# Spreading the first norm's weight row by a product, and loading and splitting the first projection's pieces in another order

## The chip, the cores and the metric

The kernel runs on one core of one Trainium2 chip. The metric is device time in microseconds of one execution; the median of several executions is compared. Lower is better.

## What is computed

A decoder trunk of two layers on 256 tokens of 1024 channels, in float32, with a final norm:

```
h = x
for i in range(2):
    hn = rmsnorm(h, ln_mix[i])
    parts = split(hn @ w_in[i])
    mix = concat(delta_rule(parts), sparse_attention(parts), stick_breaking(parts))
    h = h + mix @ w_out[i]
    h = h + conv_ffn(rmsnorm(h, ln_ffn[i]))
    h = h + sigmoid(rmsnorm(h, ln_ple[i]) @ w_ple_gate[i]) * rmsnorm(p[i] @ w_ple[i], ple_norm[i])
return rmsnorm(h, ln_final)
```

Here `rmsnorm(x, w)` is x times (mean of x² + 1e-6) to the power -1/2, times the weight row w. The change lies in the first norm of the first layer and in the first product behind it.

## The kernel before

Tokens lie on the partitions, in two tiles of 128 (`h[:, 0]` and `h[:, 1]`). Every large product is made of two summands for each operand in the format float32r: the high one is a rounded copy (written by ScalarE, `wh_...`, `XH`), the low one what is left (by VectorE, `wl_...`, `XL`), and three products of the four are summed in PSUM: high by high, low weights by XH, high weights by XL.

Weights stream in pieces (`PIECES`) through SyncE's DMA queue into five buffers (`prefetch`, L506; `WR`, L384). `split_step` (L537) splits half a piece at a time: an activation to `hi`, a subtraction to `lo`. A buffer is free, and the next piece's load is issued, when a piece is split. The first four pieces of a layer are `g1` (`wr_g` in the profile, 414 KB each, two of the eight k-tiles of the first projection each); three pieces `k` and two `kcvc` follow.

`setup` (L612) issues the first transfers on SyncE in this order: x's first tile in two halves, 160 columns of constants (the identity for the transposes among them), the weight row of the first norm spread over 128 partitions (`row(0)`, L680, 512 KB), two pieces, x's second tile, the positions, and the pieces that still have a buffer. `warm` (L632) issues products of zeros, whose results nobody reads; `WARM` holds their numbers: 12 at the start, 2 behind the first transposes, 3, 5, 5 and 0 behind the products of the four pieces.

`main` (L1774) then writes the first norm down: `norm_stats` squares a tile on ScalarE and takes (sum + eps) to the power -1/2 on GpSimd (`ssq`), `norm_mul` (L718) multiplies h by it and by the row on VectorE (`xh`), `norm_T` (L767) transposes four k-tiles on TensorE and splits them to `XH` and `XL`. `split_to(n)` stands between these steps and so sets where the pieces' splits stand on ScalarE's and VectorE's queues. `proj` (L852) takes the first projection for tile 0 of the tokens: for each piece the products with XH, then behind all four those with XL; then `second()` brings tile 1's transposes, and the same is done for tile 1.

The order of all instructions is fixed when the program is built. Each engine takes its own in order. In the mixers (the three mixers' streams) a rough model of the engines' clocks (`Model`, L191) picks what is written next, so a change of what stands ahead also changes how the streams are woven later. All computing instructions have line L307, that of the helper that records them; so they are told apart by the names of their tiles.

Of the kernel before, what the change touches and what calls it, by code (L numbers as in the profile page):

```python
# [18 lines left out]
T = 256  # L19
D = 1024  # L20
# [8 lines left out]
LAG = 2  # how many steps of the feed-forward the down-projection runs behind  # L29
LAST = 4  # pieces of the down-projection at the end, through which the tiles of tokens go one after the other  # L30
PG = [NJ - 11, NJ - 9, NJ - 7, NJ - 5]  # the steps of the feed-forward that the first pieces of the last gate come with
# the mixers' outputs (0: delta rule, 1: stick-breaking, 2: sparse) in the order in which each layer's output projection takes them
GROUPS = ((2, 0, 1), (2, 0, 1))
TILES = (3, 2, 3)  # their sizes

# columns of w_in, as the reference splits them
# [5 lines left out]
def _pieces():  # L42
    """The pieces in which the weights of a layer stream in: name, [k, columns]. w1k and w1v are used as they are."""
# [23 lines left out]
# columns of per-channel parameters  # L67
# [8 lines left out]
# columns of constants  # L76
# [8 lines left out]
CC_F = CC["lev"][0]  # from here on they are wanted in bfloat16 only  # L85
# [51 lines left out]
def _prep(inp):  # L137
    """Lays the arrays out: the weights in the order in which they stream, parameters of channels as columns."""
# [14 lines left out]
    for l in range(DEPTH):  # L153
# [16 lines left out]
        for n, i, k, c in PIECES:  # L170
            a = whole[n]
            per = a.shape[1] // k  # pieces along the contraction
            ki, ci = (i % per, i // per)
            ws.append(np.ascontiguousarray(a[:, ki * k:ki * k + k, ci * c:ci * c + c]).reshape(-1))
# [16 lines left out]
class Model:  # L191
    """A rough clock of each engine, from which the order of the instructions is chosen as they are written down."""

    HOP = {"pe": 0.2, "act": 0.16, "dve": 0.16, "pool": 0.12}
    WINDOW = 4096 / 1200  # us
    BUSY = 3060  # columns of all rows

    def __init__(self):
        self.clock = {"pe": 0.0, "dve": 0.0, "act": 0.0, "pool": 0.0}
        self.ready = {}  # L200
        self.used = {}
        self.loaded = 2.0  # when the loads so far have passed
        self.grids, self.fresh, self.banks = {}, {}, {}
        self.part = None  # the tile of tokens that is worked on
        self.parted = set()  # tensors that are followed by tiles of tokens
        self.cols = {}  # columns that the tensor engine's array passed in each window of its clock's gate

    def keys(self, names):
        """What a tensor is known by: its parts, where it is followed in parts."""
# [8 lines left out]
    def slow(self, t):  # L218
        """Whether the array runs at half its rate at a time."""
        return self.cols.get(int(t / self.WINDOW) - 1, 0.0) < self.BUSY  # L220

    def behind(self):
        """Whether the array has been too idle in this window to keep its rate in the next."""
# [4 lines left out]
    def region(self, ap):  # L228
        """When each element that an operand covers was written and was last used, as views: [half of the partitions, ...]."""
        t = ap.tensor  # L230
        if t.name not in self.grids:
            n = int(np.prod(t.shape[1:]))
            self.grids[t.name] = g = np.zeros((2, 2, n))  # (ready, used)
# [10 lines left out]
    def load(self, ap, cost):  # L244
        """A load of a piece of weights."""
# [4 lines left out]
    def op(self, eng, cost, outs, ins, cols, oaps, iaps):  # L250
# [7 lines left out]
        for b in banks:  # one engine at a time  # L258
# [24 lines left out]
class Engine:  # L283
    """Passes instructions on and counts what they cost."""
# [26 lines left out]
    def cost(self, op, out, ins, kw):  # L311
        n = max([out.free_size()] + [a.free_size() for a in ins])
        if self.n == "pe":
# [4 lines left out]
            if dt == F32:  # products for different halves of the columns run side by side in part  # L318
# [19 lines left out]
class Pool:  # L338
    """A pool of tiles whose model knows when their places were last used."""
# [19 lines left out]
class Halves:  # L359
    """One summand of a piece in several tiles, one behind the other along the contraction."""  # L360
# [8 lines left out]
class Need:  # L369
    """What a stream waits for: banks of PSUM, tiles or flags, a time."""  # L370
# [5 lines left out]
class Trunk:  # L376
    # How each layer's streams are woven together. pace: the share of columns below which the projections go first, early: how
    # long the array waits for what is more urgent, slack: how far ahead of the products the pieces are split, beside the mixers
    # and beside the feed-forward, step: k-tiles between two looks at what is more urgent; the rest: the streams' urgency.
# [4 lines left out]
    WR = 5  # pieces loaded ahead  # L384
    WARM = (12, 2, 3, 5, 5, 0)

    def __init__(self, ctx, tc, I, out, tap=None, depth=DEPTH):
# [13 lines left out]
        self.WS = 4  # pieces in two summands at a time  # L401
# [8 lines left out]
        # weights  # L410
# [6 lines left out]
        self.hold = False  # no split now: the engines have something more urgent  # L417
# [86 lines left out]
    # Pieces that are used as they are go where the mixers have nothing yet.  # L504
# [32 lines left out]
    AHEAD = (0, 1, 1, 2, 2, 1, 1, 0)  # pieces that are split behind each part of the last gate  # L537
    HALF = 512

    def split_step(self):  # L540
        """Splits half of the next piece into two float32r summands; false where there is no room."""
# [20 lines left out]
        self.a.activation(part(hi), src[:, s], AF.Copy)  # L562
        self.v.tensor_sub(part(lo), src[:, s], part(hi).bitcast(F32))
# [1323 lines left out]
```

## Time and profile before

| | |
|---|---|
| median of three runs | 847.37 us |
| lowest, highest | 846.48, 849.69 us |
| profiled execution: its span, from the first to the last instruction | 844.7 us |
| profiled execution: its own time | not stated apart; the median lies 2.7 us above the span |
| instructions | 17700 |
| TensorE, VectorE, ScalarE, GpSimd busy | 98%, 75%, 57%, 9% |
| mean granted clock of TensorE | 0.995 of full |

The profile is one execution. A row of the timeline gives start and duration in us from the start of the span, the engine (PE is TensorE, PEld its weight loads, DVE VectorE, ACT ScalarE, POOL GpSimd, SP SyncE; a q behind it is the engine's queue), the operation, the tile written and those read, and in brackets the idle time of the engine before it and what ended that. PE is "busy" whenever a product is in it, one of zeros too. PEclk is the granted clock of TensorE as a share of 2.4 GHz; 0.50 is 1.2 GHz.

### The profile page before, as it was taken

How to read it: one execution, taken by the hardware profiler on the slowest of the kernel's cores; microseconds unless marked ns; L12 is line 12 of the kernel's file. 1: busy time of each engine (PE TensorE's matmuls, PEld its weight loads, DVE VectorE, ACT ScalarE, POOL GpSimd, SP SyncE). 2: the span in 40 equal slices, each digit the busy share in tenths (PEclk: the TensorE clock that was granted, in tenths of full speed). 3: DMA queues.
4: the chain of work that ended last, by engine and by line, in shares of the span. 5: the costliest groups of instructions: out<-in, count | busy, mean ns of one | idle time of the engine just before them, and what ended most of it. 6: DMA issues, size and time to landing. Idle time of an engine off the chain costs nothing.

```text
span 844.7 us, 17700 instructions
## 1 busy us (share of the span) xinstructions
PE 827.0 (98%) x7007; PEld 742.9 (88%) x7007; DVE 633.3 (75%) x1305; ACT 480.7 (57%) x1043; POOL 77.1 (9%) x147
## 2 busy tenths in 40 slices
PE   8999999999999999999999999999999999999996
PEld 4987888987999999998999888897889999999986
DVE  4777987676887788877675688967588877878755
ACT  4546565565765566654655365637466656656543
POOL 1130001121100000000311100031110000000012
PEclk9999999999999999999999999999999999999998
DMA  8853221314575566753466133213355656766511
GB/s 283 298 189 100 77 75 41 104 58 144 198 232 191 188 211 215 224 187 120 127 227 224 34 126 102 64 52 101 126 174 196 206 197 194 215 216 213 177 35 50
DMA packets 37683, 130.71 MB, mean 155 GB/s; under 512 B 4576, under 2 KB 5088, under 8 KB 37600
## 3 DMA queue, kind: packets, MB, share of 16 engines
q1 hardware_dynamic: 36144, 124.66, 45.0%
q0 software_dynamic: 1312, 4.72, 1.7%
q8 instruction: 55, 0.90, 0.4%
q14 instruction: 28, 0.23, 0.1%
q10 hardware_dynamic: 144, 0.20, 0.1%
HBM read 128.51 MB, written 1.05 MB: 153 GB/s over the span
## 4 chain that ended last, share of the span: by engine, by line
PE 92%; ACT 3%; DMA 2%; DVE 1%; issue 0%; POOL 0%; SPq 0%; POOLq 0%; DVEq 0%; ACTq 0%
PE b L307 92%; DMA wr_w1k<-in_w_dram 1%; DMA row<-in_rows_dram 1%; ACT XH L307 1%; DMA wr_w1v<-in_w_dram 0%; DVE wl_g L307 0%; ACT L425 0%; ACT L L307 0%; ACT xh L307 0%; DVE xh L307 0%; DVE ck L307 0%; ACT cv L307 0%; POOL ssq L307 0%; ACT th L307 0%; ACT P L307 0%
## 5 line engine op out<-in xcount | busy, mean ns | idle before, releaser
L307 DVE SCALAR_TENSOR_TENSOR u<-b,pc,u 128x255 f32<-128x255 f32 (+1 forms) x176 | 84.7, 481 | 41.3 <-ACT u L307 38.2
L307 PE MATMUL b<-XL,wh_up 128*128 128x256 f32 x352 | 99.7, 283 | 0.0
L307 PE MATMUL b<-XH,wl_up 128*128 128x256 f32 x352 | 99.6, 283 | 0.0
L307 PE MATMUL b<-XH,wh_up 128*128 128x256 f32 x352 | 99.6, 283 | 0.0
L307 PE MATMUL b<-XH,wh_ga 128*128 128x256 f32 x352 | 99.0, 283 | 0.0
L307 PE MATMUL b<-XH,wl_ga 128*128 128x256 f32 x352 | 99.0, 283 | 0.0
L307 PE MATMUL b<-XL,wh_ga 128*128 128x256 f32 x352 | 97.2, 283 | 0.0
L307 ACT ACTIVATE u<-b,pc 128x256 f32<-128x256 f32 x88 | 41.6, 472 | 74.9 <-PE b L307 74.9
L307 PE MATMUL b<-wh_dn,al 128*128 128x512 f32 x176 | 69.4, 394 | 0.0
L307 PE MATMUL b<-wl_dn,ah 128*128 128x512 f32 x176 | 69.3, 394 | 0.0
L307 PE MATMUL b<-wh_dn,ah 128*128 128x512 f32 x176 | 69.2, 393 | 0.0
L307 PEld LDWEIGHTS b<-XH,wh_ga 128*128 128x128 f32 x352 | 66.9, 190 | 1.7
L307 PEld LDWEIGHTS b<-XL,wh_ga 128*128 128x128 f32 x352 | 65.9, 190 | 1.5
L307 PEld LDWEIGHTS b<-XL,wh_up 128*128 128x128 f32 x352 | 67.1, 191 | 0.0
L307 PEld LDWEIGHTS b<-XH,wh_up 128*128 128x128 f32 x352 | 67.1, 191 | 0.0
L307 PEld LDWEIGHTS b<-XH,wl_up 128*128 128x128 f32 x352 | 67.1, 191 | 0.0
L307 PEld LDWEIGHTS b<-XH,wl_ga 128*128 128x128 f32 x352 | 66.9, 190 | 0.1
L307 DVE TENSOR_TENSOR wl_ga<-wr_ga,wh_ga 128x512 fp32r<-128x512 f32 x88 | 56.9, 688 | 6.2 <-ACT wh_ga L307 2.6
L307 DVE TENSOR_TENSOR wl_up<-wr_up,wh_up 128x512 fp32r<-128x512 f32 x88 | 56.6, 685 | 0.4
L307 DVE TENSOR_TENSOR wl_dn<-wr_dn,wh_dn 128x512 fp32r<-128x512 f32 x88 | 56.6, 684 | 0.4
L307 ACT ACTIVATE ah<-sg 128x256 fp32r<-128x256 f32 x44 | 18.4, 419 | 64.7 <-DVE sg L307 64.7
L307 ACT ACTIVATE wh_up<-wr_up 128x512 fp32r<-128x512 f32 x88 | 50.3, 621 | 0.0
(371 smaller groups left out, 2243.0 us busy)
## 6 DMA issues: line engine op xcount, KB each, us to landing
wr_ga<-in_w_dram SPq DMA_DIRECT2D x44, 512.0 KB, 4.1
wr_up<-in_w_dram SPq DMA_DIRECT2D x44, 512.0 KB, 4.2
wr_dn<-in_w_dram SPq DMA_DIRECT2D x44, 512.0 KB, 3.8
wr_out<-in_w_dram SPq DMA_DIRECT2D x16, 512.0 KB, 3.5
wr_pg<-in_w_dram SPq DMA_DIRECT2D x16, 512.0 KB, 4.0
wr_g<-in_w_dram SPq DMA_DIRECT2D x8, 512.0 KB, 6.4
row<-in_rows_dram POOLq DMA_DIRECT2D x8, 512.0 KB, 4.2
wr_g<-in_w_dram SPq DMA_DIRECT2D x8, 414.0 KB, 5.0
```

The costliest lines, as they stand in the source:

```text
L307: return f(*args, **kw)
```

## The change

The row of the first norm is loaded as one row of 4 KB on one partition, by GpSimd's queue. A matrix product of a column of 128 ones by that row, one for each half of its columns, spreads it over the partitions in two banks of PSUM, which `norm_mul` then reads. The constants move from SyncE's queue to ScalarE's. All four pieces of `g1` are issued ahead of x's second tile. Products of zeros are left at two places: 3 at the start, 4 behind the two row products. The first piece is split by VectorE (high) and GpSimd (low), ahead of the first `norm_mul`; the second piece behind it, the third behind tile 0's transposes, the fourth behind tile 1's squares. In `proj` the products of the first three pieces with XL come ahead of those of the fourth piece with XH.

```diff
-    WARM = (12, 2, 3, 5, 5, 0)
+    WARM = (3, 4)
...
-    def split_step(self):
+    def split_step(self, hi_on=None, lo_on=None):
...
-        self.a.activation(part(hi), src[:, s], AF.Copy)
-        self.v.tensor_sub(part(lo), src[:, s], part(hi).bitcast(F32))
+        if hi_on is None:
+            self.a.activation(part(hi), src[:, s], AF.Copy)
+        else:
+            hi_on.tensor_copy(part(hi), src[:, s])
+        (lo_on or self.v).tensor_tensor(part(lo), src[:, s], part(hi).bitcast(F32), op=OP.subtract)
...
+        r0 = cp.tile([1, D], F32, tag="row", name="row0")
+        self.gdma(r0, I["rows"][0:1])
         for s in self.HS:
             self.sync.dma_start(self.h[:, 0, s], I["x"][0:128, s])
         cst = cp.tile([128, CC_F], F32, name="cst")
-        self.sync.dma_start(cst[:, 0:160], I["const"][:, 0:160])
-        self.row(0)
-        self.prefetch(2)
+        self.adma(cst[:, 0:160], I["const"][:, 0:160])
+        self.prefetch(4)
         self.sync.dma_start(self.h[:, 1], I["x"][128:256])
...
+        ones = self.gp.tile([1, 128], F32, tag="S", name="ones", bufs=2)
+        v.memset(ones, 1.0)
         self.warm(0)
+        self.row0 = [self.bank("row0") for _ in self.HS]
+        for b, s in zip(self.row0, self.HS):
+            self.t.matmul(b, ones, r0[:, s], start=True, stop=True)
+        self.n_row = 1
+        self.warm(1)
...
         for s in cols:
-            self.v.scalar_tensor_tensor(xh[t][:, s], self.h[:, t, s], sq[:, 0:1], row[:, s], op0=OP.mult, op1=OP.mult)
+            gains = row[s.start // 512] if isinstance(row, list) else row[:, s]
+            self.v.scalar_tensor_tensor(xh[t][:, s], self.h[:, t, s], sq[:, 0:1], gains, op0=OP.mult, op1=OP.mult)
...
         for t in range(2):
+            late = 0
             for i in range(4):
                 if t == 0:
                     Ws.append(self.take("g1", i))
+                if i == 3:
+                    yield self.need(0, self.of(t))
+                    for late in range(3):
+                        self.projB(g1[t][:, :414], X, Ws[late], t, 2 * late, range(2), 1)
                 for k in range(2):
-                    yield self.need(0, Ws[i][1], self.of(t))
+                    yield self.need(0, Ws[i][1], f"{X[0].tensor.name}/{t}")
                     self.projB(g1[t][:, :414], X, Ws[i], t, 2 * i, [k], 0)
-                if l == t == 0:
-                    self.warm(i + 2)
-            for i in range(4):
-                self.projB(g1[t][:, :414], X, Ws[i], t, 2 * i, range(2), 1)
-                if t == 1:
+            self.projB(g1[t][:, :414], X, Ws[3], t, 6, range(2), 1)
+            if t == 1:
+                for i in range(4):
                     self.done()
...
         sq = [self.norm_stats(xh, 0)]
-        self.norm_mul(xh, 0, self.rows[0], sq[0])
-        self.split_to(1)
+        self.split_to(1, hi_on=self.v, lo_on=self.g)
+        self.norm_mul(xh, 0, self.row0, sq[0])
+        self.split_to(2)
         late = []
         for k in (0, 4):
             yield from self.norm_T(xh, 0, k, late)
-        self.warm(1)
-        self.split_to(2)
+        self.split_to(3)
         sq.append(self.norm_stats(xh, 1))
         for f in late:
             f()
-        self.split_to(3)
-        self.norm_mul(xh, 1, self.rows[0], sq[1])
+        self.split_to(4)
+        self.norm_mul(xh, 1, self.row0, sq[1])
+        self.free(*self.row0)
         self.split_to(5)
```

The instructions stand so on the engines. SyncE's queue at the start, before (`h` is x, `wr_g` a piece of the first projection, numbers are those of buffers):

```order
L617 DMA h<-in_x_dram 128x512 x2
L619 DMA cst<-in_const_dram 128x160
L686 DMA row_84<-in_rows_dram 128x1024
L530 DMA wr_g_86<-in_w_dram 128x828
L530 DMA wr_g_88<-in_w_dram 128x828
L622 DMA h<-in_x_dram 128x1024
L624 DMA pos<-in_pos_dram 128x4
L530 DMA wr_g_93<-in_w_dram 128x828
L530 DMA wr_g_95<-in_w_dram 128x828
L530 DMA wr_k<-in_w_dram 128x1024 x3
```

and now, with the row (on GpSimd) and the constants (on ScalarE) gone from it and all four pieces ahead of x's second tile:

```order
L624 DMA h<-in_x_dram 128x512 x2
L530 DMA wr_g_86<-in_w_dram 128x828
L530 DMA wr_g_88<-in_w_dram 128x828
L530 DMA wr_g_90<-in_w_dram 128x828
L530 DMA wr_g_92<-in_w_dram 128x828
L628 DMA h<-in_x_dram 128x1024
L630 DMA pos<-in_pos_dram 128x4
L530 DMA wr_k<-in_w_dram 128x1024 x3
```

Two rows are gone from the queue, and the third and fourth piece stand three and four places earlier.

VectorE from its first multiplication to tile 1's, before (`xh` is h normalised, `wl_g` a piece's low summand, `XL` that of the transposed tokens):

```order
L307 SCALAR_TENSOR_TENSOR xh_118<-h,ssq,row_84 128x512 x2
L307 TENSOR_TENSOR wl_g_128<-wr_g_86,wh_g_127 128x414 x2
L307 TENSOR_TENSOR wl_g_151<-wr_g_88,wh_g_150 128x414
L307 TENSOR_TENSOR wl_g_152<-wr_g_88,wh_g_150 128x414
L307 TENSOR_TENSOR XL<-b,XH 128x4x128 x2
L307 TENSOR_TENSOR wl_g_168<-wr_g_93,wh_g_166 128x414
L307 TENSOR_TENSOR wl_g_169<-wr_g_93,wh_g_167 128x414
L307 SCALAR_TENSOR_TENSOR xh_119<-h,ssq,row_84 128x512 x2
```

and now, where the casts of the first piece stand ahead of the first multiplications, its subtractions are gone to GpSimd, and the fourth piece's subtractions have moved ahead of tile 1's multiplications (behind them before):

```order
L307 CAST wh_g_127<-wr_g_86 128x414 x2
L307 SCALAR_TENSOR_TENSOR xh_120<-h,ssq,row_109 128x512
L307 SCALAR_TENSOR_TENSOR xh_120<-h,ssq,row_110 128x512
L307 TENSOR_TENSOR wl_g_138<-wr_g_88,wh_g_137 128x414
L307 TENSOR_TENSOR wl_g_139<-wr_g_88,wh_g_137 128x414
L307 TENSOR_TENSOR wl_g_160<-wr_g_90,wh_g_158 128x414
L307 TENSOR_TENSOR wl_g_161<-wr_g_90,wh_g_159 128x414
L307 TENSOR_TENSOR XL<-b,XH 128x4x128 x2
L307 TENSOR_TENSOR wl_g_177<-wr_g_92,wh_g_175 128x414
L307 TENSOR_TENSOR wl_g_178<-wr_g_92,wh_g_176 128x414
L307 SCALAR_TENSOR_TENSOR xh_121<-h,ssq,row_109 128x512
L307 SCALAR_TENSOR_TENSOR xh_121<-h,ssq,row_110 128x512
```

Two casts have come in at the head, two subtractions have left for GpSimd, and the fourth piece has passed tile 1's multiplications.

TensorE at the end of tile 0's first projection, before, behind five products of zeros (`wh_g_178` to `wl_g_181` are the fourth piece, `cst` holds the identity):

```order
L307 MATMUL b<-wh_g_178,XH 128x414
L307 MATMUL b<-wl_g_180,XH 128x414
L307 MATMUL b<-wh_g_179,XH 128x414
L307 MATMUL b<-wl_g_181,XH 128x414
L307 MATMUL b<-wh_g_127,XL 128x414 x2
L307 MATMUL b<-wh_g_150,XL 128x414 x2
L307 MATMUL b<-wh_g_166,XL 128x414
L307 MATMUL b<-wh_g_167,XL 128x414
L307 MATMUL b<-wh_g_178,XL 128x414
L307 MATMUL b<-wh_g_179,XL 128x414
L307 MATMUL b<-cst,xh_119 128x128 x8
```

and now, where the first three pieces' products with XL stand ahead of the fourth piece's (`wh_g_175` to `wl_g_178`), so that six products follow that piece's split before tile 1's transposes where there were twelve:

```order
L307 MATMUL b<-wh_g_127,XL 128x414 x2
L307 MATMUL b<-wh_g_137,XL 128x414 x2
L307 MATMUL b<-wh_g_158,XL 128x414
L307 MATMUL b<-wh_g_159,XL 128x414
L307 MATMUL b<-wh_g_175,XH 128x414
L307 MATMUL b<-wl_g_177,XH 128x414
L307 MATMUL b<-wh_g_176,XH 128x414
L307 MATMUL b<-wl_g_178,XH 128x414
L307 MATMUL b<-wh_g_175,XL 128x414
L307 MATMUL b<-wh_g_176,XL 128x414
```

The six products with XL of the first three pieces have passed the four of the fourth piece with XH.

## Rows read from the trace of the kernel before

**Rows 1.** The page's busy times.
```profile
PE 827.0 (98%) x7007; PEld 742.9 (88%) x7007; DVE 633.3 (75%) x1305; ACT 480.7 (57%) x1043; POOL 77.1 (9%) x147
```

**Rows 2.** Waits of the first 30 us (engine, line, waited for: total, times, longest).
```profile
DVE xh L307 <- DMA row<-in_rows_dram: 7.1, 1, 7.1
```

**Rows 3.** The chain that ended last, whole span: start, duration, what.
```profile
2.10 6.00 DMA row<-in_rows_dram
8.23 0.76 DVE xh L307
9.04 0.66 PE b L307 x4
...
20.91 4.04 PE b L307 x21
```

**Rows 4.** Timeline, 0 to 45 us: start, duration, engine, line, operation.
```profile
1.21 5.27 PE L307 MATMUL b<-z 128*128 128x512 bf16 x12 [1.21 <-DVE z L307]
...
9.33 0.99 ACT L307 ACTIVATE wh_g<-wr_g 128x414 fp32r<-128x414 f32 x2 [4.52 <-DMA wr_g<-in_w_dram]
9.70 0.72 PEld L307 LDWEIGHTS b<-cst,xh 128*128 128x128 f32 x4 [0.24 <-DVE xh L307]
...
10.22 1.23 ACT L307 ACTIVATE XH<-b 128x512 fp32r<-128x512 f32 x2
...
12.93 1.28 DVE L307 TENSOR_TENSOR XL<-b,XH 128x512 fp32r<-128x512 f32 x2
...
16.58 1.08 DVE L307 TENSOR_TENSOR wl_g<-wr_g,wh_g 128x414 fp32r<-128x414 f32 x2
...
18.11 1.68 PE L307 MATMUL b<-wh_g,XL 128*128 128x414 f32 x8
...
19.62 1.04 PE L307 MATMUL b<-cst,xh 128*128 128x128 f32 x8
```

**Rows 5.** Windows: stretch, length, busy time (count) by engine, PEclk, DMA share, GB/s.
```profile
9.20:10.20 1.00, 0.99 (x7) 0.76 (x7) 0.73 (x2) 0.87 (x2) 0.00 (x0) 0.76 1.07 418
...
12.20:13.20 1.00, 1.00 (x4) 0.47 (x3) 1.00 (x3) 1.00 (x4) 0.00 (x0) 0.53 1.04 425
13.20:14.20 1.00, 1.00 (x6) 0.83 (x5) 1.00 (x3) 1.00 (x4) 0.47 (x2) 1.00 0.96 384
```

**Rows 6.** DMA issues (KB, us to landing): whole span; last line, 26 to 30.5.
```profile
h<-in_x_dram SPq DMA_DIRECT2D x2, 256.0 KB, 2.8
...
pT<-in_pT_dram POOLq DMA_DIRECT2D x2, 256.0 KB, 2.9
...
row<-in_rows_dram POOLq DMA_DIRECT2D x1, 512.0 KB, 7.4
```

**Rows 7.** Timeline of TensorE, 63 to 64.5 us.
```profile
63.20 0.81 PE L307 MATMUL b<-r,cst 128*128 128x384 f32 x2
...
64.01 0.81 PE L307 MATMUL b<-r,cst 128*128 128x384 f32 x2
```

**Rows 8.** Groups by form, VectorE and GpSimd: count, busy us, mean ns, idle before.
```profile
L307 DVE SCALAR_TENSOR_TENSOR ple<-b,pssq,row 128x512 f32<-128x512 f32 x8 | 5.6, 747 | 2.7 <-POOL pssq L307 2.7
...
L307 DVE CAST KH<-KH 64x512 fp32r<-64x512 f32 x4 | 1.7, 422 | 0.1
...
L307 POOL TENSOR_TENSOR qr<-qr,ropet 128x384 f32<-128x384 f32 x4 | 4.0, 1010 | 29.7 <-DVE ropet L307 29.7
```

**Rows 9.** Timeline, 26.5 to 28.5 us, VectorE and GpSimd.
```profile
27.24 0.86 POOL L307 CAST mb<-mst 128x800 bf16<-128x800 f32 x1 [0.77 <-DMA mst<-in_const_dram]
...
27.31 1.11 DVE L307 COPY cos<-cos 128x128 f32<-128x128 f32 x1
```

**Rows 10.** Windows, 120 to 130 us (columns as in rows 5).
```profile
120.00:130.00 10.00, 9.17 (x102) 7.82 (x100) 9.17 (x22) 8.11 (x14) 0.91 (x2) 1.00 0.28 82
```

**Rows 11.** The chain, whole span, around 121 to 128 us.
```profile
121.80 1.14 ACT wh_sk L307 x2
...
127.49 0.85 ACT P L307 x2
```

More of the change, by code (lines that the diff above doesn't have):

```diff
@@ L583, in spare, with split_to @@
         return (n, i) in self.SPARE
-    def split_to(self, n):
+    def split_to(self, n, **on):
         while self.n_split < n:
-            assert self.split_step()
+            assert self.split_step(**on)
     def split_some(self):
@@ L685, in row @@
             j = self.n_row if self.n_row < 4 * self.depth else 4 * DEPTH
-            (self.sync.dma_start if i == 0 else self.gdma)(t, self.I["rows"][j:j + 1].to_broadcast([128, D]))
+            self.gdma(t, self.I["rows"][j:j + 1].to_broadcast([128, D]))
             self.rows[self.n_row] = t
```

## The prediction

> **What bounds the kernel now.** The page comes first: TensorE is busy 98% of the span [rows 1], so the end moves only with TensorE's work or with its idle time. The waits of the first 30 us come second: VectorE sits 7.1 us until the weight row of the first norm has landed [rows 2]. The chain of waits then shows that this is no idle time of a bystander: the row's transfer, issued at 2.10, ends the chain's first 8.1 us, and the multiplication behind it starts at 8.23 [rows 3]. The timeline gives the rest [rows 4]. TensorE, "busy" from 1.21, multiplies zeros until 6.5. It transposes tile 0 of the tokens from 9.04, works through the first projection in step with the splits (the fourth piece's second summand ends at 17.66) with 15 more products of zeros in between, takes eight late products from 18.11, transposes tile 1 at 19.62 [rows 4] and starts tile 1's products at 20.91, the chain's next long stretch of TensorE [rows 3]. That is the mark: TensorE has work from there on, so what the change takes off 20.91 comes off the end, if the pieces that follow are split early enough.
>
> The granted clock [rows 5] fell from full to half within 9.2 to 10.2 (mean 0.76), after TensorE had had nothing from 6.5 to 9.0, and came back at the end of 12.2 to 13.2 (mean 0.53, then 1.00): at 13.1, about 4.1 us after work had begun again at 9.04. The first products of zeros, 12 in 5.27 us, take 0.43 each for 512 columns, which is the 1.2 GHz level, so a product of 414 columns takes 0.35 there; at 2.4 GHz they follow each other by 0.19 (eight from 18.11 to 19.62). A transpose takes 0.18 at the low level (four weight loads in 0.72 from 9.70) and 0.13 at the high one (eight in 1.04 from 19.62) [rows 4].
>
> **The change, part by part.** All times are estimates on the profiled execution's scale.
>
> *Loads.* x's first half is issued as before, the second of its two parts at 1.2, takes 2.8 us [rows 6] and is there at 4.1; the steps to 1/rms stay as they were and ended before the row did [rows 2]. The 512 KB spread row no longer stands in SyncE's queue, and all four pieces go ahead of x's second half. The engines move 384 to 425 GB/s [rows 5], so a piece of 414 KB takes 1.05 us and the four land at 5.2, 6.2, 7.3, 8.3; x's second half follows with 1.3 us at 9.6. The constants on ScalarE's queue leave at 2.0, after the table load and in the 1.4 us in which ScalarE waits for x anyway, and are wanted only by the transposes at 8.5. On GpSimd the row's issue stands ahead of the first step to 1/rms, which can't begin before 4.1; VectorE's new memset of ones ends before anything waits. None of the three costs anything while x lands at 4.1.
>
> *The row on one partition.* It leaves GpSimd at 0.8. The trace has no transfer of 4 KB from there. Below, it is bounded by pT, 256 KB on that queue in 2.9 us [rows 6], less 0.6 us for its bytes: 2.3. Above, by the spread row on that queue among full loads: 7.4. I take 2.6, next to pT, since nothing else is on that queue: 3.4 (ends 3.1 and 8.2). The Trainium skill ("DMA: Bandwidth & Descriptors", Anatomy of one DMA) gives such a transfer about 2.0 us plus its bytes; that would put it at 2.8 and the sum 0.6 us lower, 842.5, an estimate by the page that no run here shows.
>
> *The row products.* A float32 product of 384 columns takes 0.64 us (from 63.20 to 64.01 stand one, in two records, and a one-pass product of as many columns that takes 384 / 2.4 GHz = 0.16, [rows 7]), so 512 columns take 0.85 at 2.4 GHz and 1.7 at 1.2. The three products of zeros ahead, from 1.21, end at 2.5. At the low level the two end at 5.1 and 6.8, the four fillers behind them at 8.5.
>
> *VectorE's chain.* The two casts now stand ahead of the multiplications: 0.36 each (422 ns for 512 columns, [rows 8]), from 5.2 to 5.9. The multiplications with a PSUM operand take 0.75 each as in [rows 8]: 6.65, and 7.55 (the second row product, 6.8). Both are done when the fillers end, so tile 0's transposes start at 8.5 and, eight times 0.18 long at the low level, end at 9.9.
>
> *GpSimd's subtraction.* 1.0 us for 384 columns [rows 8], so 1.1 each: 8.2 at the latest, wanted at 9.9. Hidden; without that cover 1.1 us.
>
> *ScalarE and VectorE up to tile 1.* The order above sets this chain. ScalarE splits piece two at 6.3 to 7.3 (0.99 for two halves), evacuates XH from 9.2 to 10.5 (0.61 each, the second half after 9.9), then splits piece three to 11.5, squares tile 1 (two of 0.62, as XH's halves of the same size) to 12.8, and splits piece four to 13.75. VectorE follows half an operation behind: piece three 11.1 to 12.2, XL (1.28) to 13.5, piece four (1.08) to 14.6, tile 1's first multiplication to 15.35 [rows 4]. x's second half, there at 9.6, is not what this waits for.
>
> *TensorE.* Products from 9.9. Fillers and transposes are work from 6.8 on, so by the 4.1 us of [rows 5] the clock is full at 10.9: three products at 0.35, the rest of the first twelve at 0.19 or as the splits come (12.2), the six XL products of pieces one to three by 13.7, four with piece four behind 14.6, its two XL products by 15.4. That and VectorE's 15.35 meet: tile 1's transposes at 15.35, tile 1's products 1.29 us later as before (19.62 to 20.91): 16.65 against 20.91, **4.26 us less**. The 20 removed products of zeros cost nothing beyond this, since they fill waits.
>
> *Behind the mark.* The next pieces move too: their buffers come free with the splits of the first four, the fourth's at 14.6 in place of 17.66 [rows 4], so their transfers start about 3 us earlier, and their splits stand behind the same steps as before. If they gain only 3 of the 4.26 us, their lead over TensorE shrinks by 1.2; the chain shows no wait for them up to 24.95 [rows 3], so I take nothing for it and leave 1.2 us in the range. The model's clocks also move, so the mixers' instructions of both layers are woven differently: I allow 1.5 us either way, about two idle times of the size that TensorE shows there, 0.83 us in 120 to 130 [rows 10].
>
> The profile's span is 844.7 us, 2.7 below the median of the runs; I keep these 2.7. 844.7 - 4.26 + 2.7 = 843.1.
>
> **The rivals.**
>
> *The clock is up early.* If the row products (one partition deep) keep the array's clock up, it is full by about 7; fillers end at 7.7, transposes at 8.75, XH at 9.4, piece four at 13.5, tile 1's products start at 15.55: 5.35 less, **842.0**. For: a product is a product in the busy rows. Against: no row here shows one so thin.
>
> *The clock is late.* If neither they nor the fillers and transposes count for much, steady work starts at 9.9 and the 4.1 us end at 14.0. Twelve products at 0.35 take 9.9 to 14.1, the other twelve end at 16.4, the start is at 17.7: 3.2 less, **844.2**. For: in [rows 5] the level fell although transposes had begun at 9.04. It is also the price of the removed fillers.
>
> *GpSimd holds VectorE.* At 27.31 VectorE's copy of 128 columns took 1.11 us beside a GpSimd cast that ran until 28.10 [rows 9]. If the first subtractions hold both multiplications so, the second ends near 9.9 and XH at 11.2 in place of 10.5: **843.7**. The Trainium skill ("SBUF — State Buffer", SBUF: two separate sides) says that the two engines lock a port pair for a whole instruction, but only against VectorE operations in a two-port mode or with two SBUF inputs. The copy agrees with that (0.3 us after the cast's end); by it the multiplications, with their row in PSUM, are not held and the time stays 843.1, so I give this rival little.
>
> *The row is late.* Every us after 3.4 delays fillers and transposes by one. At 5.5, 2.1 us: **845.2**. From about 7.7 on the change gains nothing. For: VectorE and TensorE now both queue behind it. Against: SyncE's queue no longer carries a spread row.
>
> *Slower: the new weave uncovers ScalarE.* At 121.80 the chain leaves TensorE for ScalarE, through table loads, until 128.3, 6.5 us in which TensorE still found projection products and idled 0.83 [rows 10, 11]. If the new order has spent those products before, up to 5.7 us more are idle: -4.26 + 5.7, **848.8**; from 4.3 uncovered us on the change loses.
>
> **How the numbers follow.** Chances: forecast 0.38, early clock 0.20, late clock 0.18, held 0.08, late row 0.08, new weave 0.08. Each has the 1.5 us of the weave about it. About 0.5%, 4.2 us, is what a measurement of this kernel can tell from no change: the forecast stands on that line. Below 843.1 fall half of the forecast, three quarters of the early clock, a fifth of the late one, a third of the held: 0.44. Above 851.6 only a new weave with two such places: 0.05. The rest, 0.51, is within. The range runs from the early clock less 1.4 to the late row and 1.4: 840.6 to 846.6, leaving out most of the weave and the tails.
>
> **What would show it.** Right: pieces landed by 5.2 to 8.3, the row by 3.4, casts at 5.2, transposes of tile 0 near 8.5, tile 1's products near 16.7, and TensorE as full from there to 60 us as before. Wrong: row products that start after 4.5, the half clock past 11, VectorE's multiplications over 1 us, or a start near 16.7 whose gain is gone by 170 us.

## The result and the profile after

The changed kernel takes 855.56 us (median, 855.17 to 856.93) against 847.12 for the kernel before in the same session: a ratio of 1.0097, 95% interval 1.0084 to 1.0109, 8.2 us **slower**. The prediction was 843.1 us, with 840.6 to 846.6 around it and a chance of 0.05 for a kernel clearly slower (above 851.6). It was wrong in sign. The profiled executions stand apart by as much: spans of 844.7 and 853.6 us.

TensorE's busy time is that of [rows 1], with 16 products less, so the 8.9 us are idle time, or time at the lower clock, somewhere. Page of the changed kernel, busy times:

```profile
PE 827.0 (97%) x6991; PEld 741.0 (87%) x6991; DVE 633.7 (74%) x1306; ACT 479.5 (56%) x1041; POOL 78.3 (9%) x150
```

**Where it went** is read from two marks in each layer: the last product of the first projection's `kcvc` pieces, behind which the mixers are woven between the projection's other products, and the last product of the output projection, which ends the mixers. The view is that of one tile's instructions on TensorE (count, durations in ns, first and last start in us). Before, layer 0 and then layer 1:

```profile
L307 PE MATMUL b<-wh_kcvc,XL x16: 281/283/283, 34.4 to 39.8; 128*128 128x256 f32 x16
L307 PE MATMUL b<-wh_out,XL x32: 388/389/397, 174.3 to 202.8; 128*128 128x512 f32 x32
...
L307 PE MATMUL b<-wh_kcvc,XL x16: 281/283/283, 446.0 to 451.4; 128*128 128x256 f32 x16
L307 PE MATMUL b<-wh_out,XL x32: 387/389/497, 584.8 to 614.4; 128*128 128x512 f32 x32
```

The changed kernel:

```profile
L307 PE MATMUL b<-wh_kcvc,XL x16: 281/282/283, 33.9 to 39.3; 128*128 128x256 f32 x16
L307 PE MATMUL b<-wh_out,XL x32: 387/392/397, 174.0 to 204.4; 128*128 128x512 f32 x32
...
L307 PE MATMUL b<-wh_kcvc,XL x16: 281/282/283, 447.5 to 452.9; 128*128 128x256 f32 x16
L307 PE MATMUL b<-wh_out,XL x32: 387/389/506, 588.7 to 623.2; 128*128 128x512 f32 x32
```

At the first mark (39.3 for 39.8) the changed kernel is 0.5 us ahead, which is all that its start won in this execution. Between the marks layer 0 takes 163.0 us before and 165.1 after, layer 1 163.0 and 170.3. The feed-forward parts behind them are equally long. So -0.5 + 2.1 + 7.3 = 8.9: the loss lies in the mixers. There the diff itself changes nothing: the gate products that it reorders end ahead of the first mark (by 25.2 and 438.8 us), and between the marks only the order that the model chose is another.

Windows of layer 1 between the marks (columns as in rows 5), before and changed, tell idle from slow:

```profile
451.40:614.40 163.00, 160.92 (x1741) 137.11 (x1740) 119.23 (x285) 87.95 (x189) 22.08 (x35) 1.00 0.30 98
452.90:623.20 170.30, 162.58 (x1740) 137.40 (x1739) 118.79 (x285) 87.92 (x190) 20.11 (x35) 0.99 0.29 94
```

TensorE's idle time is 7.7 us for 2.1, and the same products keep it busy 1.7 us longer: 5.6 + 1.7 = 7.3. In layer 0 idle time makes 1.9 of the 2.1 us.

**The start** itself went its own way too. Timeline of the changed kernel, 0 to 22 us:

```profile
1.21 1.46 PE L307 MATMUL b<-z 128*128 128x512 bf16 x3 [1.21 <-DVE z L307]
1.25 0.74 POOL L622 DMA_DIRECT2D row<-in_rows_dram  x1 [0.82 <-POOLq L1896]
...
6.70 3.75 PE L307 MATMUL row<-row,ones 1*128 1x512 f32 x4 [4.03 <-DMA row<-in_rows_dram]
7.47 0.66 DVE L307 CAST wh_g<-wr_g 128x414 fp32r<-128x414 f32 x2 [6.20 <-DMA wr_g<-in_w_dram]
...
7.93 2.15 POOL L307 TENSOR_TENSOR wl_g<-wr_g,wh_g 128x414 fp32r<-128x414 f32 x2 [1.68 <-DVE wh_g L307]
...
8.96 0.75 DVE L307 SCALAR_TENSOR_TENSOR xh<-h,ssq,row 128x512 f32<-128x512 f32 x1 [0.83 <-PE row L307]
...
10.38 1.89 PE L307 MATMUL b<-z 128*128 128x512 bf16 x4
10.54 0.75 DVE L307 SCALAR_TENSOR_TENSOR xh<-h,ssq,row 128x512 f32<-128x512 f32 x1 [0.83 <-PE row L307]
...
12.06 1.80 PE L307 MATMUL b<-cst,xh 128*128 128x128 f32 x8
...
19.15 1.29 PE L307 MATMUL b<-cst,xh 128*128 128x128 f32 x8
...
20.46 0.46 PE L307 MATMUL b<-wh_g,XH 128*128 128x414 f32 x1
```

VectorE's wait of 7.1 us for the row [rows 2] has become one of 4.03 us on TensorE. The row, 4 KB, is not there before 6.70; its products run at the 1.2 GHz level (3.75 us for both); and the multiplications wait for them one by one, to 8.96 and 10.54. The transposes still take 0.22 each, the low level. Tile 1's products start at 20.46, against 20.91 in [rows 3].

**Layer 1's loss** has its largest part near 590 us. Windows (columns as in rows 5), of the kernel before:

```profile
580.00:590.00 10.00, 8.67 (x53) 6.21 (x52) 7.36 (x16) 9.68 (x20) 1.50 (x2) 1.00 0.41 147
590.00:600.00 10.00, 10.00 (x58) 8.15 (x57) 5.72 (x12) 4.95 (x11) 0.22 (x2) 1.00 0.31 105
```

and of the changed kernel:

```profile
580.00:590.00 10.00, 9.74 (x70) 7.81 (x70) 6.79 (x16) 7.02 (x15) 1.53 (x2) 1.00 0.53 158
590.00:600.00 10.00, 5.76 (x23) 3.97 (x23) 4.64 (x9) 5.25 (x11) 1.52 (x2) 0.83 0.17 54
```

The changed kernel's timeline of TensorE there, and its chain that ended last:

```profile
589.52 0.39 PE L307 MATMUL b<-wh_out,XL 128*128 128x512 f32 x1
593.84 0.85 PE L307 MATMUL b<-cst,o 128*128 128x128 f32 x3 [3.92 <-DVE XL L307]
```

```profile
591.55 0.85 ACT L L307
592.40 0.02 issue
592.42 0.94 ACT L L307
593.36 0.48 ACT XH L307
...
593.86 0.62 DVE XL L307
```

The projection's last products (`sv`) end at 584.7. From there TensorE has only what the stick-breaking mixer's chain (`L`) and the sparse mixer's last tile (`o`) give it. ScalarE works on these one after the other: it squares that tile at 589.78, between the two halves of the chain, and the tile's norm then goes through VectorE and GpSimd until 593.2. TensorE stands still for 3.92 us in one piece, and the granted clock falls (0.83 in the window, 1.00 before and behind it). In the kernel before, the longest wait for `XL` there is 0.9 us, and both of the sparse mixer's tiles are transposed at about the time at which the projection's products end (580.2):

```profile
579.99 0.49 PE L307 MATMUL b<-cst,o 128*128 128x128 f32 x3
...
581.49 0.49 PE L307 MATMUL b<-cst,o 128*128 128x128 f32 x3
```

A second place lies between 530 and 550 us, where TensorE waits 2.0 us for ScalarE's `P` and before not at all. And layer 0's loss looks like the one near 590: behind the last `sv` product (170.4) the chain runs through ScalarE's `L` again, and TensorE waits 1.87 us for what comes of it:

```profile
177.67 0.50 PE L307 MATMUL b<-wh_out,XH 128*128 128x512 f32 x1 [1.87 <-DVE XL L307]
```

### The profile page after: what moved, and what is told of

It reads as the page before. It is cut to its first block, busy times and chain, and to the rows that moved or that the text cites. A ratio compares the mean times of both kernels' runs of the same rounds, so it can differ in the third digit from the quotient of the medians.

```text
span 853.6 us, 17684 instructions
## 1 busy us (share of the span) xinstructions
PE 827.0 (97%) x6991; PEld 741.0 (87%) x6991; DVE 633.7 (74%) x1306; ACT 479.5 (56%) x1041; POOL 78.3 (9%) x150
## 4 chain that ended last, share of the span: by engine, by line
PE 84%; DVE 7%; ACT 6%; DMA 2%; issue 1%; POOL 0%; POOLq 0%; SPq 0%; ACTq 0%; DVEq 0%
PE b L307 83%; ACT L L307 1%; ACT XH L307 1%; DMA wr_g<-in_w_dram 1%; DMA row<-in_rows_dram 1%; DVE wl_g L307 1%; DVE cv L307 0%; DMA wr_w1v<-in_w_dram 0%; PE row L307 0%; DVE cq L307 0%; DVE ck L307 0%; DVE XL L307 0%; DVE mx L307 0%; DVE xh L307 0%; DVE R L307 0%
```

## The experiments

The kernel chooses the order of the mixers' instructions while it is written down: `drive` takes the stream that its `Model`'s clocks hold ready. The theory was that **the start gains a little and the order costs the rest**; the rival, that the new start does harm later on, through its loads, banks or the clock. The change touches both at once, so the order was read out of each kernel and put into the other. From the moment at which `start(0)` spawns the mixers, a list gives for each step the stream, the number of half pieces split by then, and the PSUM bank:

```diff
 def drive(self):
...
+            if self.phase in ORDER:
+                goal, u = next(self.todo)
+                while self.steps < goal and self.split_step():
+                    pass
+                s = self.uid[u]
...
+                s.append([self.bank() for _ in range(s[3].banks)])
+                self.step(s)
+                continue
             self.split_some()
```

With its own list the changed kernel comes out as it was, instruction by instruction on every engine. The list does not touch the gate products: they keep the order of the kernel that it is put into.

The two kernels and all twelve runs (medians in us; the stretch of a layer is that between the two marks above, from the profiled execution, which alone can stand 2 us off the median):

| run | median | ratio to before | first `wh_k` product | layer 0 | layer 1 |
|---|---|---|---|---|---|
| before | 847.1 | 1 | 25.5 | 163.0 | 163.0 |
| the changed kernel | 855.56 | 1.0097 [1.0084, 1.0109] | 25.1 | 165.1 | 170.3 |
| new_start_old_order | 844.89 | 0.9975 [0.9966, 0.9985] | 23.8 | 163.1 | 163.0 |
| old_start_new_order | 857.61 | 1.0126 [1.0112, 1.0140] | 25.3 | 164.6 | 171.6 |
| old_order_layer_0 | 852.84 | 1.0075 [1.0061, 1.0088] | 24.2 | 164.9 | 170.6 |
| old_order_layer_1 | 847.81 | 1.0009 [1.0000, 1.0018] | 24.6 | 166.1 | 162.9 |
| g1_order_undone | 854.17 | 1.0085 [1.0071, 1.0100] | 23.3 | 172.2 | 163.1 |
| model_clock_shifted | 863.37 | 1.0191 [1.0178, 1.0204] | 25.1 | 172.2 | 171.2 |
| before_model_shifted | 856.10 | 1.0110 [1.0095, 1.0124] | 25.5 | 172.2 | 163.1 |
| row_on_scalar_queue | 842.43 | 0.9946 [0.9934, 0.9958] | 21.4 | 163.1 | 163.0 |
| fillers_till_row | 843.03 | 0.9960 [0.9947, 0.9973] | 20.9 | 163.4 | 163.0 |
| scalar_queue_and_fillers | 842.04 | 0.9950 [0.9934, 0.9966] | 20.6 | 163.3 | 163.0 |
| fillers_between_rows | 842.80 | 0.9959 [0.9944, 0.9973] | 25.3 | 163.2 | 163.0 |
| multiplications_ahead_of_casts | 842.67 | 0.9949 [0.9937, 0.9961] | 21.4 | 163.2 | 163.0 |

### Start or order

**new_start_old_order**: `ORDER` holds both layers' lists of the kernel before, in the changed kernel.

> The changed start, and from the moment at which the mixers' streams are spawned the order of instructions (and the choice of PSUM banks) of the kernel before, read from a list instead of chosen by the kernel's own model. Theory (the loss is the order that the model chose for the mixers, the start itself gains 0.45 us): 847.1 - 0.4 = 846.7 us, between 846.0 and 847.5; out_proj of layer 1 as long as before (31 us, not 35). Rival (the start does harm later on, by its loads, banks or the clock): 855, as the changed kernel.

844.89 us. The whole loss is gone, and both layers take as long as before. The rival falls. The gain is larger than expected, 2.1 us instead of 0.4. The 0.4 had been read from one execution of the changed kernel, in which the row came late (6.70); here the row's products start at 5.11 and `wh_k`'s at 23.8.

**old_start_new_order**: the kernel before with the changed kernel's lists.

> The start of the kernel before, and from the spawning of the mixers on the order and banks of the changed kernel, read from a list. Theory (the order alone): 855.6 + 0.4 = 856.0 us, between 855 and 857. Rival (the start does harm later on): 847.

857.61 us, 0.6 above the range that was expected, and slower than the changed kernel by the start's gain. So the start gains about 2.1 us (1 to 0.9975) to 2.5 (1.0126 to 1.0097), and the order costs about 10.3 us (0.9975 to 1.0097) to 10.7 (1 to 1.0126).

**old_order_layer_0** and **old_order_layer_1**: the changed start, one layer's list from each kernel.

> The changed start; layer 0 in the order of the kernel before, layer 1 in the order of the changed kernel. Theory (each layer's order has its own price, 2.1 us in layer 0 and 7.3 in layer 1 by the marks of the two traces): 855.6 - 2.1 = 853.5 us. Rival (layer 1 is slow because of what layer 0 hands it, such as pieces split or loaded late): 846 to 848.

> The changed start; layer 0 in the order of the changed kernel, layer 1 in the order of the kernel before. Theory (each layer's order has its own price): 855.6 - 7.3 = 848.3 us. Rival (layer 1 is slow because of what layer 0 hands it): 855.

852.84 and 847.81 us: each within 0.7 us of the theory. Layer 1's order is dear whatever layer 0 did, and the two prices add up. In old_order_layer_0's profiled execution layer 0 took 164.9 us although its order is that of before. TensorE's waits there are those of new_start_old_order to within 0.2 us, but the granted clock reads 0.83 in the window from 60 to 70 us, where it reads 1.00 in that run; this execution took 854.75 us.

### Why the order changed

Of the model's state where the mixers are spawned, two things decide. Its clocks of TensorE, VectorE and ScalarE stand 0.174 us lower than in the kernel before, all three alike (TensorE's 16.587 for 16.761), which shifts them against the grid of stretches by which the model guesses the array's clock. And the gate products `g1` stand in another order for tile 1 and in layer 1. With both put back, the changed kernel comes out in the order of before in all 1763 steps; with GpSimd's clock alone, which differs by 3.1 us, nothing changes. (This is read from the programs as they are written down.) So two more orders could be had without touching any list.

**g1_order_undone** undoes the second cause:

```diff
 for t in range(2):
+    if l == t == 0:
         late = 0
...
+    else:
+        for i in range(4):
+            if t == 0:
+                Ws.append(self.take("g1", i))
+            for k in range(2):
+                yield self.need(0, Ws[i][1], self.of(t))
+                self.projB(g1[t][:, :414], X, Ws[i], t, 2 * i, [k], 0)
+        for i in range(4):
+            self.projB(g1[t][:, :414], X, Ws[i], t, 2 * i, range(2), 1)
+            if t == 1:
+                self.done()
```

> The changed kernel with one part undone: outside the first tile of layer 0 the first projection takes its products in the order of the kernel before (the residual products of the second summand of X last). The order of the mixers is chosen by the model again; in layer 1 it comes out as in the kernel before but for 10 of 875 steps, in layer 0 it is a third order (178 steps of 888 go to another stream). Theory (the price is that of each layer's order, whatever its cause): layer 1's 7.3 us are gone, 855.6 - 7.3 = 848.3 us, give or take 2 for the third order of layer 0. Rival (the loss hangs on the new start): 855.

854.17 us, 6 more than expected. Layer 1 is as in the kernel before (163.1), as the theory said. Layer 0's third order takes 172.2 us, 9.2 more than before's, where 2 had been allowed. That each layer's order has its own price holds; that a new order costs about 2 us does not.

**model_clock_shifted** undoes the first:

```diff
 def start(l):
     self.hold = False
+    if l == 0:
+        self.M.off = -0.174
 def slow(self, t):
-    return self.cols.get(int(t / self.WINDOW) - 1, 0.0) < self.BUSY
+    return self.cols.get(int((t - self.off) / self.WINDOW) - 1, 0.0) < self.BUSY
```

(`off` is subtracted alike in `behind` and `op`.)

> The changed kernel with the model's windows of the array's clock laid 0.174 us earlier from the spawning of the mixers on, which is how far the model's own clocks at that place stand apart in the two kernels; no instruction is added or taken away, but the order comes out anew in both layers. Theory (the orders scatter by several us and the model does not see it): it differs from 855.6 by more than 1.5 us, one way or the other, most likely between 846 and 854. Rival (the model knows what it does, and orders that it chooses at nearly equal clocks are nearly equal in time): 855 to 856.

863.37 us, 7.8 slower than the changed kernel by no instruction more or less. The sign of the expectation's "most likely" was wrong, the scatter larger still.

**before_model_shifted** is the same line in the kernel before, with +0.174; its order from the spawning on is that of g1_order_undone:

> The kernel before with its model's windows of the array's clock laid 0.174 us later from the spawning of the mixers on, and nothing else: no instruction is added or taken away, the start is that of before. The order comes out as in g1_order_undone (a third one in layer 0, before's but for ten steps in layer 1). Theory (each layer's order has its own price: 172.2 us from the last kcvc product to the last of out_proj in g1_order_undone's layer 0, 163.0 before): 847.0 + 9.2 = 856.2 us, between 855 and 857.5. Rival (the third order was dear only behind the new start): 847 to 849.

856.10 us, forecast 856.2. One tile's view, layer 0 (the first mark stands at 39.8 as before):

```profile
L309 PE MATMUL b<-wh_out,XL x32: 388/389/628, 177.4 to 212.0; 128*128 128x512 f32 x32
```

A shift of 0.174 us in a clock that exists only while the program is written down makes the kernel before 9 us slower. None of the four orders that the same model chose for a layer in these kernels is quicker than its own. What makes one order dearer than another was only read, not tried: near 590 us and in layer 0 of the changed kernel (above), and in this third order, where TensorE's longest wait in layer 0 is again one for `XL`, 3.3 us, behind the same chain.

### What the start can give

All five keep the order of the kernel before by list, so that the start is measured alone.

**row_on_scalar_queue**:

```diff
-        self.gdma(r0, I["rows"][0:1])
+        self.adma(r0, I["rows"][0:1])
```

> The changed start with the order before read from a list (the kernel of the first experiment), and the row issued on ScalarE's queue ahead of the constants instead of on GpSimd's. Theory (the row lands late because of its queue; the constants landed 3.0 to 3.1 us behind an issue at 0.76): the row lands at about 3.9 instead of 5.1 to 6.7; VectorE's multiplications then wait for the first pieces' casts ahead of them on its queue, no longer for the second row product, so some 1 to 1.6 us of the lead is won: 843.3 to 843.9. Rival 1 (a row on one partition is slow on any queue): 844.9, row at 5 or later. Rival 2 (the pieces set the pace): 844.6 to 845, row at 3.9.

842.43 us, 2.5 us less than new_start_old_order and 0.9 less than the best that was expected. Timeline:

```profile
0.76 0.51 ACTq L684 DMA_DIRECT2D row<-in_rows_dram  x1
...
2.60 3.78 PE L310 MATMUL row<-row,ones 1*128 1x512 f32 x4
6.31 1.89 PE L310 MATMUL b<-z 128*128 128x512 bf16 x4
8.03 1.97 PE L310 MATMUL b<-cst,xh 128*128 128x128 f32 x8
...
11.72 0.55 PE L310 MATMUL b<-wl_g,XH 128*128 128x414 f32 x1
12.06 0.46 PE L310 MATMUL b<-wh_g,XH 128*128 128x414 f32 x1
12.36 0.35 PE L310 MATMUL b<-wl_g,XH 128*128 128x414 f32 x1
...
16.82 0.46 PE L310 MATMUL b<-wh_g,XH 128*128 128x414 f32 x1 [0.25 <-ACT XH L310]
```

The row's products start behind the fillers without any wait: it was there by 2.60, at most 1.84 us after its issue at 0.76. On GpSimd's queue the same 4 KB took 3.4 to 5.3 us from issue to landing in six profiled executions. Both rivals fall. The edit changes two things at once, though: the queue, and the time of the issue, 0.76 in place of 1.25, ahead of the pieces' loads at 1.63. Which of them makes the row quick was not tried apart. The multiplications now wait for the casts ahead of them (first piece at 6.66), as expected.

**fillers_till_row**:

```diff
-    WARM = (3, 4)
+    WARM = (9, 4)
```

> The kernel of the first experiment with nine products of zeros ahead of the row's products instead of three, so that TensorE works through most of its wait for the row. Theory (the row's products run at half the clock because TensorE rested before them): granted clock full before or within the row's products, which then take about 1.9 us and not 3.75, and the transposes come up to 2 us earlier: 842.9 to 844. Rival (the clock falls back, or the extra products delay the row's as often as they help): 844.5 to 845.5.

843.03 us, some 1.3 to 1.9 less than new_start_old_order, but the two intervals overlap and its eleven executions lie between 841.97 and 846.61 us, so the size of the gain stays open. In the profiled one the row's products took 1.95 us instead of 3.75. The first gate products still ran at the low level (0.55 each up to 11.3).

**scalar_queue_and_fillers**: both edits.

> The kernel of row_on_scalar_queue with nine products of zeros ahead of the row's products, as in fillers_till_row. Theory (both gains are of the same few microseconds, and the pieces, landing at 6.1 to 6.7, are next): the row's products start right behind the fillers at 5.0 at the full clock, in every execution, the multiplications behind the casts at 6.7: 841.5 to 842.3. Rival (no gain beside either alone): 842.4 or more.

842.04 us: within the forecast, but its interval overlaps that of either edit alone, so the second gain is not shown. It has the lowest median of all (by the ratio row_on_scalar_queue is as low) and beats the kernel before by 0.34 to 0.66%, and with it the changed kernel. The full clock did not come "in every execution": one of six took 846.36 us, and in the profiled one the row's products took 2.36 us, between the 1.95 and the 3.75 seen above. Its first microseconds:

```profile
1.21 4.02 PE L310 MATMUL b<-z 128*128 128x512 bf16 x9 [1.21 <-DVE z L310]
5.16 2.36 PE L310 MATMUL row<-row,ones 1*128 1x512 f32 x4
7.45 1.04 PE L310 MATMUL b<-z 128*128 128x512 bf16 x4
8.32 1.04 PE L310 MATMUL b<-cst,xh 128*128 128x128 f32 x8
```

**fillers_between_rows**:

```diff
-    WARM = (9, 4)
+    WARM = (9, 1, 3)
             self.t.matmul(b, ones, r0[:, s], start=True, stop=True)
+            self.warm(2)
```

> As scalar_queue_and_fillers, with three products of zeros behind each of the two row products and one instead of four ahead of the transposes. Theory (the clock falls behind the row's products because these use one row of the array only): it stays up, the transposes take about 1.0 us instead of 1.7 to 2.0 and the first products 0.35 instead of 0.55: 840.5 to 841.5. Rival (it falls with the transposes all the same, and the second multiplication comes some 0.3 us later): 842 to 842.6.

842.80 us, not told apart from the others: inconclusive on what holds the clock up. Its profiled execution, one that took 846.42 us, shows why one execution cannot tell:

```profile
1.21 4.02 PE L310 MATMUL b<-z 128*128 128x512 bf16 x9 [1.21 <-DVE z L310]
5.16 2.07 PE L310 MATMUL row<-row,ones 1*128 1x512 f32 x2
...
12.23 1.85 PE L310 MATMUL b<-cst,xh 128*128 128x128 f32 x8
```

The same nine fillers at the same times as above, and this time the low level lasted to 13.98.

**multiplications_ahead_of_casts**:

```diff
+        self.norm_mul(xh, 0, self.row0, sq[0])
         self.split_to(1, hi_on=self.v, lo_on=self.g)
-        self.norm_mul(xh, 0, self.row0, sq[0])
```

> As scalar_queue_and_fillers, with the first tile's two multiplications ahead of the first piece's casts on VectorE. Theory (the casts, waiting for a piece that lands at 6.1 to 6.7, hold the multiplications up): multiplications at 6.5 instead of 7.2, the transposes 0.3 to 0.7 us earlier, but the first piece's second summand 0.8 later, from 9.3 at the latest: 841.3 to 842. Rival (the first piece's summands become the wait): 842.3 to 843.

842.67 us: no gain. The multiplications came at 6.55 as expected and the transposes at 7.64 instead of 8.32, but the fourth gate product then waited 0.73 us for the first piece's second summand, and tile 1's transposes came at 15.47 instead of 14.73. The rival was right: there the pieces set the pace.

## Why the prediction was wrong

**The step that failed** is the one on the weave: "I allow 1.5 us either way, about two idle times of the size that TensorE shows there". It was 9.4 us in the profile (2.1 and 7.3), and 10.3 to 10.7 by the exchanged orders. Its yardstick was an idle time of the order that stood there [rows 10]; but a new order is no disturbance of the old one, it is drawn anew. Four orders of layer 0 and layer 1 that the same model chose lie between 163 and 172 us a layer.

**The slower rival** had the kind of wait that the trace shows: ScalarE at work with none of the projection's products left to cover it. It looked for it at 121.8 to 128.3 us in layer 0 [rows 11]; there TensorE did not idle at all between 120 and 130. It came at the end of the mixers, 1.87 us up to 177.67 in layer 0 and 3.92 us from 589.91 in layer 1. The rival priced one place at up to 5.7 us, and was given 0.08. That the diff also reorders layer 1's gate products, which feed the same model, is not in the prediction.

**The start's -4.26 us** was over-sized: 2.1 to 2.5 us in the medians, 0.45 in the profile, where tile 1's products start at 20.46 and not at 16.65. One of its terms is at fault for most of that, and two more were wrong without costing much here.
- The row was to leave at 0.8, take 2.6 us and land at 3.4 (ends 3.1 and 8.2). It was issued at 1.25 and took 5.3 us: there at 6.70, and at 4.76 to 6.69 in the five other profiled executions with this start. These 3.3 us are nearly all of the 3.8 that were missing. The nearest row was pT's at 2.9 us; the landings lie between it and the upper bound. The experiment bears this out: with the row there by 2.60 (row_on_scalar_queue), tile 1's products start at 16.82. The Trainium skill ("DMA: Bandwidth & Descriptors", Anatomy of one DMA) gives about 2.0 us for such a transfer on GpSimd's path; the traces disagree there (3.4 to 5.3), and what was measured beneath 2.0 came over ScalarE's queue (at most 1.84).
- The first piece was to land at 5.2. It was there at 7.47 (6.1 to 8.0 in the other profiled executions). In this execution its casts ended at 8.13, and the multiplication behind them waited for the row's product until 8.96.
- The clock was to be full at 10.9. Transposes at 12.06 still had the low level, products at 13.81 the full one. The transposes had been planned at the low level, at 0.18 each; they took 0.22, which with the row's products makes up the rest of the 3.8 us.

In the chances, the four shares that fall below 843.1 add up to 0.40 and not to the 0.44 that stands there.

**What held**: the row's two products, 3.75 us against 3.4; the multiplications, 0.75 us each; GpSimd's subtractions, 1.07 us each. While the second of these ran (to 10.08), the first multiplication took its usual 0.75 from 8.96, so the rival by which GpSimd holds VectorE is out. The Trainium skill ("SBUF — State Buffer", SBUF: two separate sides) has the two engines shut each other out only where VectorE's operation is in a two-port mode or has two SBUF inputs; the trace agrees. The late-row rival had the right cause; at its 5.5 us it forecast a gain of 2.1, and new_start_old_order gained 2.1 with the row there by 5.11. And row_on_scalar_queue, where the row comes even ahead of the plan and the order is held, takes 842.43 us: about what was forecast for the change.

## What to carry to other kernels

Where a program chooses its own order by estimated clocks, any edit ahead of the choice draws a new order, and the spread of orders (here 844.89 to 863.37 us behind the same start) can drown what the edit is worth. Before judging such an edit, write down the old order and replay it, or exchange orders between the two versions; and see whether the old version keeps its time when its model is shifted by a fraction of a microsecond. A small transfer that everything waits for should be issued early, over a queue whose small transfers the trace has shown to be quick.

## What was not expected of the hardware

The same 4 KB to one partition: 3.4, 3.7, 4.3, 4.7, 5.3 and 5.3 us on GpSimd's queue in executions with the same start, at most 1.84 us on ScalarE's.

TensorE's clock at the start varies by microseconds. In row_on_scalar_queue TensorE had work without a pause from 1.21 and stayed at the 1.2 GHz level until 12.06; with nine fillers it was at 2.4 GHz from the products of zeros at 7.45 on in one execution and at 1.2 GHz until 13.98 in another, from the same instructions up to 7.16. The Trainium skill ("TensorE: Matmul & The Clock Gate", Part 1: The HAM clock gate) says that the length of this slow stretch differs between runs of one kernel. These two executions agree, but they lie more than 6 us apart, and the page gives 0.5 us either way. In the windows of these stretches the granted clock reads 1.00 while the durations show the low level, so at the very start of a trace the level is better read from durations.
